# A one-core encoder layer in split precision: layer-norm fillers dealt anew, scratch sums on other memory, a fixed load order between up and down projection, and the last token tiles finished in halves

## The chip, the core and the metric

One core of one Trainium2 chip runs the whole layer. The metric is the device time of one execution in microseconds, the median of several. TensorE does the matrix products, VectorE (DVE), ScalarE (ACT) and GpSimd (POOL) the rest, and DMA queues, most of them SyncE's (SP), move data between the memories.

## What is computed

The reference is one layer of a streaming encoder for 1024 prompt tokens and 64 sample tokens of width 1024, in float32:

```python
u = x * (1.0 + sc1) + sh1
xr, gl, q, k, v, ga, gb = split(u @ w_in)              # 1024 -> 7 x 1024
y_a = RG_LRU(causal_conv4(xr)) * gelu(gl)
y_b = chunk_band_attention(q, k, v)
merged = sigmoid(ga) * y_a + sigmoid(gb) * y_b
x1 = LN(ALPHA * x + (1.0 + g1) * (merged @ w_out))
u2 = x1 * (1.0 + sc2) + sh2
f = square(relu(u2 @ w_up + b_up)) @ w_down + b_down   # 1024 -> 4096 -> 1024
y = LN(ALPHA * x1 + (1.0 + g2) * f)
```

The outputs are y of both token sets, the newest keys and values, and the recurrent states. The change touches what follows `merged`.

## The kernel before

Every matrix product is made of three: each operand is split into a high part (ACT, a copy to the rounded format) and a low part (VectorE, the difference), and `mm3` (lines 108 to 111) adds high by high, high by low and low by high. The tokens are cut into three groups: groups 0 and 1 of 384 prompt tokens, and group 2 of 256 prompt and 64 sample tokens (320 columns).

**First layer norm.** `outproj` (541) multiplies `merged` by w_out in eight blocks of 128 features. `ln1` (583) takes a group's three tiles of tokens: `ln1_a` transposes a tile (tile `rt`), makes its statistics and normalizes it on ACT (tile `n1`); `ln1_b` transposes it back (tile `nt`), makes u2 in high and low parts (`u2h`, `u2l`) and, on GpSimd, the part that the second norm adds (`nT`). Between the steps `fill(i)` puts other matmuls: the output projection of the next group, dealt by `cut` (642), and in group 2 the first blocks of the up projection, dealt by `early` (652). The power of -0.5 in the statistics (522) runs on GpSimd.

**Up projection.** 32 feature blocks go in 16 pairs. Pairs 0 and 1 are made within the layer norm, in plain form, their results in `hr`; pair 2 is plain too. From pair 3 on, groups 0 and 1 go through a Strassen scheme of seven products (`strassen`, 742) whose token operands are u2 and four sums of it, T1 to T4. These sums are made on VectorE in `tt` tiles (684 to 705): joins of high and low parts, subtractions, then splits into the T tiles. `wops` (708) makes the sums of weights on GpSimd and their splits. Group 2 is plain (`up_g2`, 754). For pairs 14 and 15 (`LATE`, 763) the second weight is split only in half, and group 2 is done after all pairs, with the weights loaded and split a second time (843 to 848).

**Down projection.** Results lie in DRAM (`hs_d` for the scheme, `hg_d` for group 2). `down_g2` (824) does group 2 for the first half of the features, then four passes c of the scheme run over seven operands each, then `down_g2` does the second half of group 2. Between its blocks stand the final norms of groups 0 and 1, one tile of tokens each (`final`, 885), and after it that of group 2.

Tiles take their memory in pools that are opened and closed; a new pool lies on the memory of closed ones, and each tile waits for those that lay there. The instructions of each engine are put in order by a planner with a timing model of its own; each engine, and each DMA queue, then takes them strictly in that order. `tc.issue_after(x)` queues the instructions of its block that run on x's engine behind x.

## Time and profile before

| | us |
|---|---|
| median of 3 runs (lowest, highest) | 1777.72 (1776.98, 1779.84) |
| the profiled execution, its own time | 1780.97 |
| its span, first to last instruction | 1779.0 |
| TensorE busy / weight loads busy | 1718.8 / 1682.1 |
| VectorE / ACT / GpSimd busy | 1012.8 / 771.4 / 457.4 |

In the profile a line names the engine, the source line, the operation and its tiles, written as out<-in. PE is TensorE, PEld its weight load. The granted clock is 1.00 at 2.4 GHz and 0.50 at 1.2 GHz; a stretch with both has a mean. A wait in brackets is the idle time of the engine ahead of the instruction and what ended it. Times within the execution are counted from its first instruction.

### The profile page before, as it was taken

The page shows a single profiled execution, that of the slowest core. Times are in us where ns is not written, and L with a number is a line of the kernel's source. Part 1 is how long each engine was busy: PE and PEld are TensorE (multiplying, and loading weights), DVE is VectorE, ACT ScalarE, POOL GpSimd, SP SyncE. Part 2 cuts the span into 40 slices and gives each one's busy share as a digit, 9 for nine tenths or more (in the row PEclk, how much of TensorE's full clock was granted, in tenths as well). Part 3 has the DMA queues.
Part 4 walks back from the last instruction along what each step waited for, and adds up shares of the span by engine and source line. Part 5 has one row for each costly group of instructions (what it writes and reads, how often), then busy time and mean ns, then how long its engine had stood idle before and what let it go on. Part 6 is the DMA issues. An engine that isn't in the chain of part 4 may idle for free.

```text
span 1779.0 us, 26773 instructions
## 1 busy us (share of the span) xinstructions
PE 1718.8 (97%) x10684; PEld 1682.1 (95%) x10684; DVE 1012.8 (57%) x1596; ACT 771.4 (43%) x1158; POOL 457.4 (26%) x487
## 2 busy tenths in 40 slices
PE   7999999999999999999999988999999899999996
PEld 4999999999999999999899888999998899999996
DVE  4594553746536374453656738333332567897876
ACT  2452543625244262443534444555555543344343
POOL 1100010000100000010025665556654024443313
PEclk8999999999999999999999999999999899999998
DMA  9241313122221122212154533333333973454343
GB/s 360 90 134 56 100 50 103 57 69 81 69 97 53 61 93 68 97 48 70 63 188 148 187 117 113 125 125 125 130 135 115 346 258 116 167 195 143 137 154 113
DMA packets 88253, 220.20 MB, mean 124 GB/s; under 512 B 11520, under 2 KB 42496, under 8 KB 88128
## 3 DMA queue, kind: packets, MB, share of 16 engines
q1 hardware_dynamic: 72512, 191.21, 31.8%
q10 hardware_dynamic: 11520, 14.69, 2.3%
q0 software_dynamic: 4096, 12.59, 1.9%
q8 instruction: 84, 1.38, 0.3%
q14 instruction: 41, 0.34, 0.1%
HBM read 173.62 MB, written 44.83 MB: 123 GB/s over the span
## 4 chain that ended last, share of the span: by engine, by line
PE 86%; DVE 5%; issue 3%; DMA 2%; ACT 2%; POOL 1%; SPq 0%; ACTq 0%; DVEq 0%; POOLq 0%
PE z L111 12%; PE z L110 12%; PE z L109 12%; PE po L402 3%; PE s L391 2%; PE xu L109 2%; PE xu L110 2%; PE xu L111 2%; PE dg L111 2%; PE dg L109 2%; PE dg L110 2%; PE xd L109 2%; PE ug L111 2%; PE xd L111 2%; PE ug L109 2%
## 5 line engine op out<-in xcount | busy, mean ns | idle before, releaser
L109 PE MATMUL z<-uh,wh_in 128*128 128x384 f32 (+1 forms) x1320 | 435.3, 330 | 2.9 <-ACT uh L102 2.9
L110 PE MATMUL z<-ul,wh_in 128*128 128x384 f32 (+1 forms) x1320 | 436.9, 331 | 0.3 <-DVE ul L103 0.3
L111 PE MATMUL z<-uh,wl_in 128*128 128x384 f32 (+1 forms) x1320 | 435.7, 330 | 0.0
L109 PEld LDWEIGHTS z<-uh,wh_in 128*128 128x128 f32 x1320 | 248.7, 188 | 6.3 <-ACT uh L102 3.9
L110 PEld LDWEIGHTS z<-ul,wh_in 128*128 128x128 f32 x1320 | 248.6, 188 | 4.4 <-DVE ul L103 2.3
L111 PEld LDWEIGHTS z<-uh,wl_in 128*128 128x128 f32 x1320 | 248.7, 188 | 4.0 <-issue 3.1
L96 ACT ACTIVATE wh_in<-wr_in 128x1024 fp32r<-128x1024 f32 x56 | 59.4, 1060 | 105.2 <-PE z L110 100.3
L97 DVE TENSOR_TENSOR wl_in<-wr_in,wh_in 128x1024 fp32r<-128x1024 f32 x56 | 68.5, 1223 | 43.2 <-ACT wh_in L96 43.1
L111 PE MATMUL dg<-ophg,wl_dg 128*128 128x320 f32 x256 | 79.3, 310 | 1.6 <-DVE wl_dg L97 1.6
L160 DVE SCALAR_TENSOR_TENSOR ap<-ar,sil,ap 128x512 f32<-128x512 f32 x112 | 79.7, 742 | 0.0
L109 PE MATMUL dg<-ophg,wh_dg 128*128 128x320 f32 x256 | 79.6, 311 | 0.0
L110 PE MATMUL dg<-oplg,wh_dg 128*128 128x320 f32 x256 | 79.1, 309 | 0.0
L451 POOL MEMSET er<- 128x1 f32 x8 | 1.1, 136 | 296.9 <-DVE rt L447 296.9
L103 DVE TENSOR_TENSOR slo_u<-sr_u,shi_u 128x1024 fp32r<-128x1024 f32 x26 | 33.0, 1267 | 65.9 <-ACT shi_u L102 65.9
L374 ACT ACTIVATE pr<-pr,st 128x640 f32<-128x640 f32 (+2 forms) x64 | 44.7, 699 | 57.7 <-DVE st L373 57.5
L103 DVE TENSOR_TENSOR opl<-op,oph 128x1536 fp32r<-128x1536 f32 x28 | 59.7, 2132 | 15.0 <-ACT oph L102 14.9
L357 DVE COPY v<-vt 128x512 f32<-128x512 f32 x16 | 11.1, 692 | 96.9 <-PE vt L356 96.9
L398 ACT ACTIVATE pts<-pt 128x512 f32<-128x512 f32 (+2 forms) x64 | 33.3, 520 | 74.2 <-PE pt L396 73.2
L102 ACT ACTIVATE shi_d<-sr_d 128x1024 fp32r<-128x1024 f32 x32 | 33.8, 1057 | 72.4 <-PE yd L110 49.7
L330 POOL TENSOR_TENSOR ko<-kh,kl 128x512 f32<-128x512 f32 x8 | 10.3, 1290 | 212.2 <-DVE kl L324 181.8
L402 PE MATMUL po<-pts,v 128*128 128x128 f32 x480 | 64.1, 275 | 0.5 <-ACT pts L398 0.3
L103 DVE TENSOR_TENSOR wlo_u<-wr_u,whi_u 128x1024 fp32r<-128x1024 f32 (+1 forms) x26 | 36.3, 1398 | 48.5 <-ACT whi_u L102 48.5
(372 smaller groups left out, 4707.9 us busy)
## 6 DMA issues: line engine op xcount, KB each, us to landing
wr_in<-in_w_in SPq DMA_DIRECT2D x56, 512.0 KB, 3.3
ar<-in_w_ada SPq DMA_DIRECT2D x46, 512.0 KB, 5.1
op<-hs_d SPq DMA_DIRECT2D x28, 768.0 KB, 5.0
wr_u<-in_w_up SPq DMA_DIRECT2D x37, 512.0 KB, 3.7
wr_dg<-in_w_down SPq DMA_DIRECT2D x32, 512.0 KB, 4.2
wr_d<-in_w_down SPq DMA_DIRECT2D x32, 512.0 KB, 4.3
wr_o<-in_w_out SPq DMA_DIRECT2D x24, 512.0 KB, 3.5
hs_d<-t POOLq DMA_DIRECT2D x64, 192.0 KB, 2.5
```

The lines of the kernel that those rows point to most:

```text
L96: S.activation(hi, raw, AF.Copy)
L97: V.tensor_tensor(lo, raw, hi.bitcast(F32), op=ALU.subtract)
L102: S.activation(hi, src, AF.Copy)
L103: V.tensor_tensor(lo, src, hi.bitcast(F32), op=ALU.subtract)
L109: TE.matmul(ps, wh, xh, start=first, stop=False, skip_group_check=more)
L110: TE.matmul(ps, wh, xl, start=False, stop=False, skip_group_check=more)
L111: TE.matmul(ps, wl, xh, start=False, stop=last, skip_group_check=more)
L160: V.scalar_tensor_tensor(part[:, w, :], raw[:, j, :], sil[:, kb, w:w + 1], part[:, w, :], op0=ALU.mult, op1=ALU.add)
L374: S.activation(pr[:rows, :W], pr[:rows, :W], AF.Exp, bias=st[:rows, 0:1], scale=-1.0, accum_out=st[:rows, 1:2])
L391: TE.matmul(sps[:, bk, :cw], qq[:, q0:q0 + P], kk[:, P * j0 + c0:P * j0 + c0 + cw], start=(ip == 0), stop=(ip == 2))
L398: S.activation(pts[:, :min(W, 512)], pt[:, :min(W, 512)], AF.Copy)
L402: TE.matmul(po[:, :P], v[:, j0 + j, :], pts[:, P * j:P * j + P], start=(j == 0), stop=(j == nk - 1))
```

## The change

1. `cut` and `early` deal the same blocks otherwise; the last piece of `early` is queued behind the last transpose of the layer norm.
2. The three `tt` tiles of the first half are asked for ahead of the T tiles, which changes the memory of both.
3. `LATE` is 15 and all weights are split whole. Pair 14 does its group 2 at once; pair 15 does it after the last product, with the weights it has. The loads around the start of the down projection are given an order, and the load of the last norm's factors goes behind the last operand.
4. In the passes of the down projection the weights of the first block are asked for ahead of the seven operands.
5. For the last three tiles of tokens the transposes and statistics of the first four features blocks are made within the last `down_g2`, three more blocks follow there, and the last one comes after it; the final operations are spread otherwise.

```diff
-        cut = ((0, 1), (2, 3), (4, 5), (6,), (7,))
+        cut = ((0,), (1, 2), (3, 4), (5, 6), (7,))
...
         def early(i):
-            for f in (ef[0:2], (), ef[2:4], ())[i] if i < 4 else ():
-                wt[f] = up_w(f)
-                up_mm(f, wt[f], 0)
-            for f in ((), ef[0:2], (), ef[2:3], ef[3:4])[i]:
-                up_mm(f, wt[f], 1)
-
-        ln1(2, rTs[2], early)
+            for k in ((0,), (1,), (2,), (3,), ())[i]:
+                wt[ef[k]] = up_w(ef[k])
+                up_mm(ef[k], wt[ef[k]], 0)
+            for k in ((), (0,), (1,), (2,), (3,))[i]:
+                up_mm(ef[k], wt[ef[k]], 1)
+
+        tail_of_ln = ln1(2, rTs[2], lambda i: early(i) if i < 4 else None)
+        with tc.issue_after(tail_of_ln):
+            early(4)
...
+        tts = [tt3(0)]
         ut = {}
...
-            x, y, z = (fp.tile([P, 2, GW], F32, tag="tt", bufs=3, name=f"tt{q}_{k}") for k in range(3))
+            x, y, z = tts.pop() if tts else tt3(q)
...
-        PLAIN, LATE = 3, 14
+        PLAIN, LATE = 3, 15
...
-            w, wa, wb = wops(a["w_up"][f1], a["w_up"][f2], f"u{p}_", p < LATE)
+            w, wa, wb = wops(a["w_up"][f1], a["w_up"][f2], f"u{p}_", True)
...
-            if p < LATE:
-                up_g2(p, wa, wb)
+            if p == LATE:
+                return wa, wb
+            up_g2(p, wa, wb)
...
         def down_g2(cs, hg, after):
...
-                        wh, wl = wsplit(a["w_down"][c, 4 * r + b], f"dg{r}_{c}_{b}")
+                        with tc.issue_after(loads[1]):
+                            wh, wl = wsplit(a["w_down"][c, 4 * r + b], f"dg{r}_{c}_{b}")
+                        if b == 1 and (c + 1, 0) not in hg and c + 1 in cs:
+                            with tc.issue_after(wlast[0]):
+                                hg.update({(c + 1, h): load_hg(c + 1, h) for h in range(2)})
+                            with tc.issue_after(loads[-1]):
+                                SY.dma_start(fg, facc_d[:, :, TS2:T])
...
-        wt = [up_w(f) for f in fblocks(LATE)]
         hg = {(0, h): load_hg(0, h) for h in range(2)}
         up_g2(LATE, *wt)
-        with tc.issue_after(loads[-1]):
-            for p in range(LATE + 1, 16):
-                up_g2(p, *(up_w(f) for f in fblocks(p)))
-        hg.update({(1, h): load_hg(1, h) for h in range(2)})
         fg = actb.tile([P, NB, TW2], F32, tag="act", bufs=2, name="fg")
-        SY.dma_start(fg, facc_d[:, :, TS2:T])
...
         for c in range(4):
-            ops = []
+            w, ops = down_w(c, 0), []
             for k in range(7):
                 o = hp.tile([P, 4, GW], F32, tag="opr", bufs=2, name=f"op{c}_{k}")
-                loads.append(SY.dma_start(o, hs_d[c, k]).ins)
+                with tc.issue_after(wloads[-1] if c == 0 and k > 4 else loads[-1]):
+                    loads.append(SY.dma_start(o, hs_d[c, k]).ins)
                 ops.append(op_split(o, f"{c}_{k}"))
...
+        with tc.issue_after(loads[-1]):
+            SY.dma_start(lg, a["ln2"][0].partition_broadcast(P))
+            SY.dma_start(lb, a["ln2"][1].partition_broadcast(P))
...
+        def final2():
+            lo, hi = halves
+            done = []
+            for c, cw, y, st, pt in g2t:
+                V.bn_stats(st[:cw, 1, :], pt[:cw, :])
+                done.append((c, cw, y, pt, *ln_moments(st, cw, f"b2_{c}")))
+            for c, cw, y, pt, mean, rstd, nb in done:
+                S.activation(y[:cw, lo], y[:cw, lo], AF.Identity, bias=nb, scale=rstd)
+                V.scalar_tensor_tensor(y[:cw, hi], pt[:cw, :], mean, lg[:cw, hi], op0=ALU.subtract, op1=ALU.mult)
+                (G if c == 0 else V).tensor_tensor(y[:cw, lo], y[:cw, lo], lg[:cw, lo], op=ALU.mult)
+                G.tensor_tensor(y[:cw, lo], y[:cw, lo], lb[:cw, lo], op=ALU.add)
+                V.scalar_tensor_tensor(y[:cw, hi], y[:cw, hi], rstd, lb[:cw, hi], op0=ALU.mult, op1=ALU.add)
+                SY.dma_start(a["y"][TS2 + c:TS2 + c + cw, :], y[:cw])
...
+        def between(r, c, b):
+            n = 8 * r + 4 * (c - 2) + b
+            if n % 2 == 1 and n < 12:
                 final(*next(fin))
+            if n == 13:
+                final2_open()
+            elif n == 14:
+                final2_more((4,))
+            elif n == 15:
+                final2_more((5, 6))
```

`final2_open` makes the transposes of feature blocks 0 to 3 of the last three tiles, their copy from the accumulators on ACT and the first half of the statistics; `final2_more(fbs)` adds the transposes of the blocks named, which `down_g2` has finished by then.

## Rows read from the trace of the kernel before

**Rows 1.** The page's busy time and share by engine.

```profile
PE 1718.8 (97%) x10684; PEld 1682.1 (95%) x10684; DVE 1012.8 (57%) x1596; ACT 771.4 (43%) x1158; POOL 457.4 (26%) x487
```

**Rows 2.** Stretches: length, busy time (instructions) by engine, PEclk, DMA share, GB/s.

```profile
1420.00:1440.00 20.00, 20.00 (x139) 20.00 (x138) 10.37 (x14) 6.80 (x7) 0.00 (x0) 1.00 0.75 264
1540.00:1560.00 20.00, 20.00 (x118) 20.00 (x117) 15.46 (x18) 5.92 (x7) 8.65 (x6) 1.00 0.30 102
988.90:996.00 7.10, 4.57 (x23) 4.38 (x22) 3.44 (x8) 3.18 (x3) 4.13 (x5) 0.76 0.62 213
1048.40:1057.20 8.80, 3.93 (x16) 3.91 (x16) 4.22 (x9) 1.64 (x3) 7.62 (x13) 0.61 0.25 80
1098.40:1109.00 10.60, 5.85 (x18) 5.09 (x19) 10.34 (x11) 6.11 (x10) 3.18 (x4) 0.68 0.44 145
1359.70:1371.00 11.30, 7.63 (x28) 6.80 (x27) 2.00 (x2) 4.55 (x8) 4.88 (x7) 0.70 0.29 104
1382.10:1395.00 12.90, 6.56 (x25) 5.90 (x24) 7.79 (x6) 9.05 (x10) 0.00 (x0) 0.60 0.83 298
1416.70:1418.60 1.90, 0.29 (x3) 0.03 (x2) 1.88 (x4) 1.52 (x2) 0.00 (x0) 1.00 0.89 350
1580.00:1640.00 60.00, 59.05 (x339) 58.35 (x338) 50.77 (x52) 25.03 (x23) 24.80 (x16) 1.00 0.47 162
```

**Rows 3.** Waits of TensorE: total us, times, longest.

```profile
PE up L109 <- ACT u2h L102: 6.3, 2, 4.9
...
PE xd L111 <- DVE wlo_d L103: 3.6, 3, 2.0
PE nt L572 <- ACT n L564: 3.2, 2, 2.5
...
PE xd L109 <- DVE facc L873: 2.5, 3, 0.9
```

**Rows 4.** Timeline (start us, us) behind the layer norm, and joins: ns min/median/max.

```profile
1047.71 0.71 PE L572 MATMUL nt<-ident,n 64*128 64x64 f32 x8
...
1053.27 0.73 DVE L103 TENSOR_TENSOR u2l<-uf,u2h 128x512 fp32r<-128x512 f32 x1 [0.69 <-ACT u2h L102]
1060.08 1.45 DVE L97 TENSOR_TENSOR wl_u<-wr_u,wh_u 128x1024 fp32r<-128x1024 f32 x1 [6.08 <-ACT wh_u L96]
...
1071.48 4.05 DVE L689 TENSOR_TENSOR tt<-u2h,u2l 128x768 f32<-128x768 f32 x2
...
L689 DVE TENSOR_TENSOR tt<-u2h,u2l x8: 945/2043/2082, 1071.5 to 1104.5; 128x768 f32<-128x768 f32 x8
```

**Rows 5.** Timeline of ACT around the last pair and the seam.

```profile
1359.91 1.06 ACT L96 ACTIVATE wh_u<-wr_u 128x1024 fp32r<-128x1024 f32 x1 [1.69 <-PE xu L110]
...
1362.55 0.49 ACT L782 ACTIVATE c<-xu 128x384 f32<-128x384 f32 x1 [0.56 <-ACT c L609]
...
1384.26 2.43 ACT L102 ACTIVATE ophg<-hg 128x1280 fp32r<-128x1280 f32 x2 [0.57 <-ACT cg L609]
```

**Rows 6.** The seam: SP's loads of hg, their landing, and TensorE's restart.

```profile
1373.33 0.82 SPq L821 DMA_DIRECT2D hg<-hg_d  x2
...
hg<-hg_d SPq DMA_DIRECT2D x2, 640.0 KB, 5.1
...
1387.69 0.63 PE L109 MATMUL ug<-u2h,wh_u 128*128 128x320 f32 x1 [5.28 <-ACT wh_u L96]
```

**Rows 7.** Timeline of the tail.

```profile
1754.73 2.42 POOL L901 TENSOR_TENSOR y<-y,lgb 128x1024 f32<-128x1024 f32 x1 [3.21 <-DVE y L900]
1760.10 2.78 PE L907 MATMUL yt<-ident,fg 128*128 128x128 f32 x24
1760.89 3.85 DVE L518 BATCH_NORM_STATS2 lstb<-yt 128x6 f32<-128x512 f32 x6
...
1768.94 1.71 POOL L901 TENSOR_TENSOR y<-y,lgb 128x512 f32<-128x512 f32 x1 [1.97 <-DVE y L900]
...
1773.49 0.68 DVE L901 TENSOR_TENSOR y<-y,lgb 64x512 f32<-64x512 f32 x1
```

More of the change, by code (lines that the diff above doesn't have):

```diff
@@ L515, in ln_stats, with ln_moments @@
             st = cpool.tile([P, 2, 6], F32, tag="lst", bufs=3, name=f"lst{nm}")
-            mv = cpool.tile([P, 6], F32, tag="lmv", bufs=3, name=f"lmv{nm}")
             for h in range(2):
                 V.bn_stats(st[:rows, h, :], ps[h][:rows, :])
+            return ln_moments(st, rows, nm)
+        def ln_moments(st, rows, nm):
+            mv = cpool.tile([P, 6], F32, tag="lmv", bufs=3, name=f"lmv{nm}")
             V.bn_aggr(mv[:rows, 0:2], flat(st[:rows]))
@@ L571, in ln1_b @@
             for fb in range(NB):
-                TE.transpose(pb[:, P * fb:P * fb + cw], n1[:cw, P * fb:P * fb + P], ident[:cw, :cw])
+                last = TE.transpose(pb[:, P * fb:P * fb + cw], n1[:cw, P * fb:P * fb + P], ident[:cw, :cw])
             nT = big([P, NB, cw], f"nT{g}_{c}")
@@ L581, in ln1_b @@
             SY.dma_start(facc_d[:, :, t0 + c:t0 + c + cw], nT)
+            return last.ins
         def ln1(g, rT, fill):
@@ L594, in ln1 @@
             fill(3)
-            ln1_b(g, n[2], *t[2])
+            last = ln1_b(g, n[2], *t[2])
             fill(4)
+            return last
         hraw = {}
@@ L678, in whole, with tt3 @@
             return x.bitcast(F32)
+        def tt3(q):
+            return [fp.tile([P, 2, GW], F32, tag="tt", bufs=3, name=f"tt{q}_{k}") for k in range(3)]
+        tts = [tt3(0)]
         ut = {}
@@ L706, in body @@
         uops = [b11, b21, ut[2], ut[1], ut[3], b22, ut[4]]
+        wloads, loads = [], []
         def wops(src1, src2, nm, full):
@@ L834, in down_g2, with down_w @@
                                 c == cs[0] and k == 0, c == cs[-1] and k == 7)
[L835 to L843 removed]
+                            if k == 4:
+                                after(r, c, b)
+                        if c == cs[-1]:
+                            fb = 4 * r + b
+                            for c0, c1, w in parts(2):
+                                fc = fg[:, fb, c0:c1]
+                                V.scalar_tensor_tensor(fc, ps[b][:, c0:c1], ada[:, G2, fb, w:w + 1], fc, op0=ALU.mult, op1=ALU.add)
         hg = {(0, h): load_hg(0, h) for h in range(2)}
         up_g2(LATE, *wt)
[L846 to L849 removed]
         fg = actb.tile([P, NB, TW2], F32, tag="act", bufs=2, name="fg")
[L851 to L852 removed]
+        down_g2((0, 1), hg, lambda r, c, b: None)
+        def down_w(c, j):
+            return wops(a["w_down"][c, 2 * j], a["w_down"][c, 2 * j + 1], f"d{c}_{j}", False)[0]
         for c in range(4):
[L855 removed]
+            w, ops = down_w(c, 0), []
             for k in range(7):
                 o = hp.tile([P, 4, GW], F32, tag="opr", bufs=2, name=f"op{c}_{k}")
[L858 removed]
+                with tc.issue_after(wloads[-1] if c == 0 and k > 4 else loads[-1]):
+                    loads.append(SY.dma_start(o, hs_d[c, k]).ins)
                 ops.append(op_split(o, f"{c}_{k}"))
@@ new lines, in body, with final @@
+        with tc.issue_after(loads[-1]):
+            SY.dma_start(lg, a["ln2"][0].partition_broadcast(P))
+            SY.dma_start(lb, a["ln2"][1].partition_broadcast(P))
+        halves = [slice(0, 512), slice(512, 1024)]
+        def final(g, i):
+            t0, tw = GROUPS[g]
+            c, cw = tok_tiles(g)[i]
+            pt = [acc(f"yt{g}_{c}_{h}") for h in range(2)]
+            for fb in range(NB):
+                TE.transpose(pt[fb // 4][:cw, P * (fb % 4):P * (fb % 4) + P], facc[fb][:, GW * g + c:GW * g + c + cw], ident)
+            y = hp.tile([P, D], F32, tag="sraw" if c < P else "slo", bufs=2, name=f"y{g}_{c}")
+            for h, s in enumerate(halves):
+                S.activation(y[:cw, s], pt[h][:cw, :], AF.Copy)
+            mean, rstd, nb = ln_stats([y[:, s] for s in halves], cw, f"b{g}_{c}")
+            S.activation(y[:cw], y[:cw], AF.Identity, bias=nb, scale=rstd)
+            V.tensor_tensor(y[:cw], y[:cw], lg[:cw], op=ALU.mult)
+            G.tensor_tensor(y[:cw], y[:cw], lb[:cw], op=ALU.add)
+            SY.dma_start(a["y"][t0 + c:t0 + c + cw, :], y[:cw])
@@ new lines, in body, with final2_open @@
+        g2t = []
+        def final2_open():
+            for c, cw in tok_tiles(2):
+                pt = acc(f"yt2_{c}_0")
+                for fb in range(4):
+                    TE.transpose(pt[:cw, P * fb:P * fb + P], fg[:, fb, c:c + cw], ident)
+                y = hp.tile([P, D], F32, tag="shi" if c < 2 * P else "opl", bufs=2 if c < 2 * P else 7, name=f"y2_{c}")
+                S.activation(y[:cw, halves[0]], pt[:cw, :], AF.Copy)
+                st = cpool.tile([P, 2, 6], F32, tag="lst", bufs=3, name=f"lst2_{c}")
+                V.bn_stats(st[:cw, 0, :], y[:cw, halves[0]])
+                g2t.append([c, cw, y, st])
@@ new lines, in final2_more @@
+        def final2_more(fbs):
+            for t in g2t:
+                c, cw = t[0:2]
+                if len(t) == 4:
+                    t.append(acc(f"yt2_{c}_1"))
+                for fb in fbs:
+                    TE.transpose(t[4][:cw, P * (fb - 4):P * (fb - 4) + P], fg[:, fb, c:c + cw], ident)
+        def final2():
[11 more added lines that the diff above has]
+                SY.dma_start(a["y"][TS2 + c:TS2 + c + cw, :], y[:cw])
@@ L932, in arrays_of @@
+        down_g2((2, 3), hg, between)
+        final2_more((7,))
+        final2()
 def arrays_of(i):
```

58 lines of the change are left out of this document (6 added, 52 removed).

## Prediction

> **What bounds the kernel now.** I read the page's totals first: TensorE is busy 97% of the span and its weight loads 95% [rows 1]. So the time is TensorE's own work plus its stops, and an edit on another engine is worth only what it takes from a stop. Then busy time by stretch [rows 2]. The first two rows give the full pitch: 20 us hold 139 matmuls of 320 columns, or 118 of 384, the ones cut by the edges counted whole; with two taken off, 0.146 and 0.172 us from one to the next. The other rows are the stops, which sit at the seams. The count of matmuls tells each loss: what that count takes at full pitch, taken from the length of the stretch.
>
> - 988.9 to 996.0: 8 transposes and some 15 matmuls, about 3.1 us of work in 7.1: 4.0 lost.
> - 1048.4 to 1057.2: 16 at 0.146 is 2.3 of 8.8: 6.5 lost.
> - 1098.4 to 1109.0: 18 at 0.172 is 3.1 of 10.6: 7.5 lost.
> - 1359.7 to 1371.0: 28 at 0.172 is 4.8 of 11.3: 6.5 lost.
> - 1382.1 to 1395.0: 25 at 0.146 is 3.7 of 12.9: 9.2 lost.
> - 1416.7 to 1418.6: 3 is 0.4 of 1.9: 1.5 lost.
>
> In all but the last the granted clock of the stretch is 0.60 to 0.76: behind these stops TensorE goes on for some microseconds at its lower level, 1.2 GHz, so a stop costs more than its idle time. The waits of TensorE add 6.1 us in the down projection (3.6 for weight remainders, 2.5 for VectorE's accumulations) and, in the first layer norm, 0.7 for n and 1.4 for u2h beside the long ones counted above [rows 3]. Together 43.4 us. Behind the last matmul stand 19 us of tail.
>
> **The change part by part.** All times are of the profiled execution: span 1779.0, its own time 1780.97, which is 3.25 above the median 1777.72. I subtract the sum from either.
>
> *Fillers, groups 0 and 1.* Eight blocks of the output projection are dealt 1, 2, 2, 2, 1 instead of 2, 2, 2, 1, 1. No instruction is added. Two blocks instead of one now stand ahead of the third tile's transposes, one block fewer ahead of the first tile's. The waits are for n and u2h [rows 3], 6.1 us in all. Both come out of a chain that passes through GpSimd's queue, and the change leaves that queue's work as it is, so I expect little: 1.5 gained, bounds -3.5 (a block of 24 matmuls at 0.146 missing ahead of the first tile) and 6.1.
>
> *Fillers, group 2.* Three of four blocks' matmuls are dealt one by one, and the last (24 matmuls of 384 columns, 4.1 us) is queued on TensorE behind the last transposes. In the trace those end at 1048.42 [rows 4] and TensorE then idles 4.9 us for u2h [rows 3], with the slow stretch behind. Work that doesn't hang on the last tile covers 4.1 of the 4.9; 0.8 idle should not lose the clock, since the 1.5 at 1416.7 did not. Gain 6.5 - 0.8 = 5.7; bounds 4.1 (the clock falls all the same) and 6.5.
>
> *Sums on other memory.* The three scratch tiles of the first half are asked for ahead of the eight T tiles, so they lie at the low end of the pool, where the layer norm's scratch (xa, n1) was, and not where the early blocks' results lay. In the trace VectorE sits idle 6.08 us ahead of 1060.08 and does weight remainders alone up to 1071.48, where the joins start, though the last of u2 was there at 1054.0 [rows 4]. From then to the last T split it is busy throughout, and TensorE waits for it: the 7.5 us. Eight joins at a median of 2.04 are 16 us; with as many subtractions and eight remainders of half a join's size or more I estimate 35 us of VectorE. Starting 10 to 15 us earlier in idle time they end ahead of the third pair. The T tiles move by 9 KB onto other results that are stored late; that may take some of the lead back. Gain 6.5, bounds 0 and 7.5.
>
> *Pair 14 regular, pair 15 keeps its weights.* LATE goes from 14 to 15 and the weights of both are split whole. Four loads of 512 KB, four ACT splits (1.06) and four VectorE remainders (1.2) go; two half splits (0.5 and 0.6) come per pair, under matmuls. At 1359.7 TensorE waits for the copy of pair 15's x (1362.55), which stands in ACT's queue behind the high part of a reloaded weight (1359.91, itself waiting for TensorE) and pair 14's last results [rows 5]. That weight split goes, and 48 matmuls of group 2 (7.0 us) stand between the two pairs, as in the pairs before, where no stop stands (from 1118 to 1342 TensorE waits for nothing). Gain 5.8 of 6.5, bounds 0 and 6.5.
>
> *The seam.* The wait of 5.3 for a reloaded weight goes with the reload. What is next: the first down matmul needs hg, and hg's load starts at 1373.33 [rows 6], when the memory of u2h of group 1 is read for the last time by pair 15; the change doesn't touch that. From there two loads land in 5.1 (median), two ACT splits take 2.43, the first weight's split 1.06 and its remainder 1.23: 9.8 us at best. TensorE holds 12 matmuls (2.1) and pair 15's group 2 (7.0): 9.1. That would leave 0.7. But in the trace ACT takes hg at 1384.26, behind the last group-2 results [rows 5], though by the median it had landed at 1378.4. With pair 15's results in the place of pair 14's, the same order gives the same restart, 14.4 us after the load [rows 6], and the same 9.2. And 7 us less of TensorE work covers the loads of hg, fg and the first weights. For it, the two lgb loads and the reloads no longer stand among them, and the order hg, two weights, hg, fg is fixed. I take the first stop as staying and the 1.5 at 1416.7 as going, with 0.5 more: gain 2.0, bounds -4 (one weight queued behind hg and fg late by one 24-matmul block) and 10.
>
> *Down projection.* Weights of j = 0 are queued ahead of the seven operands. VectorE is busy 50.8 of 60 us there [rows 2] (the last row), with peaks at each operand change. The order moves, the work stays: gain 2.0 of 6.1, bounds -2 and 6.1.
>
> *The tail.* 21 of 24 transposes move in among the matmuls; at 2.78 us for 24 [rows 7] that puts the last matmul 2.4 later. Three half tiles of statistics remain of six (3.85): 1.9 less. Then VectorE's rest falls by some 2.5 us, but GpSimd gets four operations of 512 columns in a row where it had two. One took 1.71 with VectorE beside it, 1024 columns took 2.42 without [rows 7]. So 4.8 to 6.8 us. I let them start at 1767.5: the first such operation of the trace, 1768.94, less two products of VectorE that it waited for, plus the later matmuls. They end at 1772.3 to 1774.3, against 1774.17 for VectorE's last of before. Gain 0.9, bounds -1 and 3. The Trainium skill (SBUF — State Buffer, SBUF: two separate sides) says that a VectorE operation with two SBUF inputs and a GpSimd one that reads SBUF exclude each other, the later one waiting whole: by it the slow figure holds wherever VectorE multiplies in SBUF, and the tail gains nothing; by the lone figure it gains 1.9. The trace's 1.71 agrees with the rule.
>
> Sum: 1.5 + 5.7 + 6.5 + 5.8 + 2.0 + 2.0 + 0.9 = 24.4. 1777.72 - 24.4 = 1753.3 (1756.6 for a run like the profiled one).
>
> **The rivals.** *The seam closes too.* If hg is split ahead of the last results, 8 more go at the seam, and with the weights early 3 more in the down projection: 1742. Against it: ACT's order in the trace. *The T tiles don't come earlier and the fillers of group 1 only move their wait*: 6.5 and 1.5 stay, 1761. For it: the T tiles' new memory also holds early results, which are stored late. *The planner deals the instructions by its own timing and most stops reappear elsewhere*: within 3 us of 1777.7. *VectorE's queue turns against TensorE, and it is slower.* With scratch memory free early, joins and T operations can stand ahead of the remainders of the weights that TensorE needs next. It has 24 matmuls at 0.172 and 72 at 0.146, 14.6 us, from the last transposes on; VectorE is free after 5.7 of them, so 9 us, or some six T operations of 1.5, fit. All 24 ahead cost 26 us, 2 more than the sum gains, with the clock lost again: 1782. It decides from some 22 operations on; the idle time ahead of the weight remainders [rows 4] speaks against so many.
>
> **How the numbers follow.** Forecast 0.56, own range 1746 to 1760. Seam closes: 0.14. T tiles late: 0.17. Nothing moves: 0.05. VectorE's queue: 0.08. Adding 0.2% (3.6 us, about what a measurement of this kernel can tell from no change) on either side of 1777.7: faster 0.56 + 0.14 + 0.17 = 0.87, same 0.05, slower 0.08. The range takes the first three, with the seam's and the down projection's bounds on the low side and the first part's and the seam's losses on the high side: 1739 to 1768.
>
> **What would show it.** No wait for u2h over 1 us behind the last transposes, and full clock there. Joins starting within 12 us of those transposes, no wait for T1l. No wait for the copy of x in the last pair. At the seam, the number that I trust least: how long after hg's load the first down matmul starts, 9 to 10 us or 14. In the down projection the waits for wlo. In the tail, GpSimd's last add against VectorE's last. Wrong would be: a new wait of TensorE for wl_u after the layer norm, or one for wl_dg several blocks into the down projection.

## The result, and the profile after

The changed kernel takes 1764.37 us (median; 1761.64 to 1767.86) against 1778.78 us of the kernel before, timed beside it: a ratio of 0.992, 95% interval 0.990 to 0.9941, so 14 us less. Forecast were 1753.3 us and 24.4 us less. The profiled execution of the changed kernel took 1761.64 us with a span of 1759.7, 2.7 below its median; the profiled one of before lies 2.2 above the median that holds here. So the spans differ by 19.3 us where the medians differ by 14.4, and what follows divides the 19.3.

The page's busy time by engine, after (before: [rows 1]). TensorE's busy time falls by 9.0 us: behind the stop at the seam a matmul of 320 columns is busy 0.47 to 0.64 us and at full clock 0.31, so time won back behind stops shows here too.

```profile
PE 1709.8 (97%) x10684; PEld 1674.2 (95%) x10684; DVE 1002.0 (57%) x1590; ACT 768.7 (44%) x1150; POOL 465.1 (26%) x489
```

TensorE's waits from 935 us to the end, after (total us, times, longest; before: [rows 3]). The wait for `u2h` is down from 6.3 to 0.8, that for `wlo_d` from 3.6 to 0.4. The wait for the high part of a weight at the seam is as long as it was: 5.2, now for `wh_dg`. The wait for `n` between the layer norm's steps is longer, 4.1 instead of 3.2.

```profile
PE dg L111 <- ACT wh_dg L98: 5.2, 1, 5.2
PE nt L577 <- ACT n L569: 4.1, 4, 2.1
PE yu L112 <- DVE T1l L105: 2.5, 1, 2.5
PE xd L111 <- DVE facc L894: 2.3, 3, 0.9
...
PE yu L111 <- ACT T1h L104: 1.0, 1, 1.0
PE up L111 <- ACT u2h L104: 0.8, 1, 0.8
...
PE xd L113 <- DVE wlo_d L105: 0.4, 1, 0.4
```

The stretches that answer to [rows 2] (length; busy time and count for PE, PEld, DVE, ACT, POOL; clock; DMA): the end of the layer norm, the T tiles, the last pair, the seam. The first and third run at full clock; the second and fourth still drop to 0.86 and 0.74.

```profile
1041.00:1050.00 9.00, 8.11 (x51) 7.26 (x50) 4.95 (x10) 3.22 (x6) 8.79 (x14) 1.00 0.32 102
1089.00:1101.00 12.00, 8.17 (x37) 7.19 (x36) 11.58 (x13) 6.59 (x12) 1.69 (x4) 0.86 0.53 166
1340.00:1366.00 26.00, 25.37 (x151) 25.05 (x151) 6.46 (x8) 12.02 (x23) 6.06 (x8) 1.00 0.20 71
1373.00:1386.00 13.00, 6.71 (x29) 6.04 (x28) 7.79 (x6) 8.54 (x10) 0.03 (x1) 0.74 0.82 287
```

As in the prediction, the loss of a stretch is its length less what its matmuls take at full pitch. At the seam: 29 matmuls less the two cut by the edges, 27 at 0.146 are 3.9 us of 13.0, so 9.1 are lost. Done in this way from matmul to matmul over the whole stage, and for the tail from the start of the 96th down matmul from the last to the end of the span:

| step | forecast gain | lost before, us | lost after, us | gain in the traces |
|---|---|---|---|---|
| fillers, groups 0 and 1 | 1.5 | 12.0 | 10.4 | 1.6 |
| fillers, group 2 | 5.7 | 8.1 | 3.2 | 4.9 |
| sums on other memory | 6.5 | 7.9 | 6.1 | 1.8 |
| pair 15 | 5.8 | 7.0 | 0.9 | 6.1 |
| seam | 2.0 | 11.5 | 9.2 | 2.3 |
| down projection, to 1660 us | 2.0 | 8.4 | 4.0 | 4.4 |
| tail (length) | 0.9 | 33.1 | 35.9 | -2.8 |

They add up to 18.3; the other 1.0 lies in places below 1 us. Two steps failed: the sums, and the tail. Two gains are less sure than the table looks. The line between the two rows of fillers is a choice: drawn at the last transposes of group 1, the first row loses as much after as before (10.0 and 9.9) and the second gains 6.6; only their sum, 6.5, doesn't depend on it. And the loss in the down projection varies by 3 us between traces of the same code (below).

**The T tiles.** VectorE's timeline, after. The joins (`tt<-u2h,u2l`) have their new memory and wait for nothing; yet they start at 1063.92, right behind the last of four weight remainders, which VectorE reached after waits of 4.7, 1.9, 2.2 and 2.3 us for their high parts.

```profile
1059.26 1.23 DVE L99 TENSOR_TENSOR wl_u<-wr_u,wh_u 128x1024 fp32r<-128x1024 f32 x1 [2.15 <-ACT wh_u L98]
1062.78 1.23 DVE L105 TENSOR_TENSOR wlo_u<-wr_u,whi_u 128x1024 fp32r<-128x1024 f32 x1 [2.30 <-ACT whi_u L104]
1063.92 2.69 DVE L702 TENSOR_TENSOR tt<-u2h,u2l 128x768 f32<-128x768 f32 x3
```

and some lines on, beside GpSimd's timeline of the same time:

```profile
1074.45 0.95 DVE L105 TENSOR_TENSOR T3l<-tt,T3h 128x768 fp32r<-128x768 f32 x1
1075.32 2.05 DVE L702 TENSOR_TENSOR tt<-u2h,u2l 128x768 f32<-128x768 f32 x1
...
1086.03 3.91 DVE L105 TENSOR_TENSOR T4l<-tt,T4h 128x768 fp32r<-128x768 f32 x1
```

```profile
1069.81 1.89 POOL L743 TENSOR_TENSOR sr_u<-wr_u,sr_u 128x512 f32<-128x512 f32 x1
1075.10 1.45 POOL L739 TENSOR_TENSOR sr_u<-wr_u 128x512 f32<-128x512 f32 x1 [3.39 <-DMA wr_u<-in_w_up]
1076.63 1.88 POOL L740 TENSOR_TENSOR sr_u<-sr_u,wr_u 128x512 f32<-128x512 f32 x1
1079.68 1.94 POOL L742 TENSOR_TENSOR sr_u<-wr_u,wr_u 128x512 f32<-128x512 f32 x1 [1.17 <-DVE slo_u L105]
```

An operation of VectorE that begins while GpSimd stands idle (1071.70 to 1075.10, 1078.51 to 1079.68) takes 0.95 us; beside GpSimd's sums the same one takes 2.05, and the one at 1086.03, beside three subtractions of GpSimd in a row, 3.91. From 1066.5 to 1089.9 nine operations together take 11.2 us longer than their undisturbed kind. TensorE is ready for T at 1090.4; the second half of `T1l` ends at 1094.7.

**The seam.** ScalarE's timeline, and the two loads of `hg` with their landing, after. `hg` had landed by 1370.6 (4.6 us, median, from issue); ScalarE takes it at 1375.88, behind the last group-2 results of pair 15, as forecast. From the load to the first down matmul (1379.31) it is 14.3 us, forecast 14.4.

```profile
1374.11 0.53 ACT L615 ACTIVATE cg<-ug,bup 128x320 f32<-128x320 f32 x1 [2.99 <-PE ug L113]
...
1375.88 2.43 ACT L104 ACTIVATE ophg<-hg 128x1280 fp32r<-128x1280 f32 x2 [0.53 <-ACT cg L616]
1378.22 2.93 ACT L98 ACTIVATE wh_dg<-wr_dg 128x1024 fp32r<-128x1024 f32 x3
```

```profile
1364.99 0.80 SPq L837 DMA_DIRECT2D hg<-hg_d  x2
```

**The tail.** VectorE's and GpSimd's timelines, and the line of the program's end with the duration of its operations in ns (min/median/max). A VectorE operation on one column of 64 rows takes 1.21 us instead of 0.14: it ends at 1748.15, when GpSimd's first product ends. GpSimd's four operations take 6.9 us and end at 1753.57, VectorE at 1750.0. Then GpSimd's drain, 8.83 us long and ending at 1758.9, holds the end: the last store had landed at 1756.6.

```profile
1746.94 1.21 DVE L528 SCALAR_TENSOR_TENSOR lmvb<-lmvb 64x1 f32<-64x1 f32 x1
```

```profile
1746.60 1.54 POOL L953 TENSOR_TENSOR y<-y,lgb 128x512 f32<-128x512 f32 x1 [1.22 <-ACT y L951]
1748.22 5.36 POOL L954 TENSOR_TENSOR y<-y,lgb 128x512 f32<-128x512 f32 x3
```

```profile
L1025 POOLq DRAIN  x3: 40/102/8832, 1750.1 to 1759.4; - x3
```

### The profile page after: what moved, and what is told of

Read it like the earlier page. It is cut to its first block, busy times and chain, and to the rows that moved or that the text cites. A ratio compares the mean times of both kernels' runs of the same rounds, so it can differ in the third digit from the quotient of the medians.

```text
span 1759.7 us, 26743 instructions
## 1 busy us (share of the span) xinstructions
PE 1709.8 (97%) x10684; PEld 1674.2 (95%) x10684; DVE 1002.0 (57%) x1590; ACT 768.7 (44%) x1150; POOL 465.1 (26%) x489
## 4 chain that ended last, share of the span: by engine, by line
PE 88%; DVE 5%; issue 2%; DMA 2%; ACT 1%; POOL 1%; SPq 0%; POOLq 0%; ACTq 0%; DVEq 0%
PE z L112 13%; PE z L113 13%; PE z L111 12%; PE po L404 3%; PE s L393 2%; PE dg L113 2%; PE dg L112 2%; PE dg L111 2%; PE xd L111 2%; PE xu L111 2%; PE xu L112 2%; PE xu L113 2%; PE xd L112 2%; PE xd L113 2%; PE ug L113 2%
## 5 line engine op out<-in xcount | busy, mean ns | idle before, releaser
L98 ACT ACTIVATE wh_in<-wr_in 128x1024 fp32r<-128x1024 f32 x56 | 59.3, 1060 | 105.3 <-PE z L112 100.3
L111 PE MATMUL ug<-u2h,whi_u 128*128 128x320 f32 x208 | 64.3, 309 | 0.0
```

Of the source, the lines that this page charges most:

```text
L98: S.activation(hi, raw, AF.Copy)
L111: TE.matmul(ps, wh, xh, start=first, stop=False, skip_group_check=more)
```

## The experiments

Ratios are to the kernel before, timed beside each; the changed kernel's is 0.992 (0.990 to 0.9941). Intervals are some 0.2% to either side, 3.5 us, so effects below that are read from the traces. In traces of the same code the loss at T lies between 5.9 and 7.4 us, that at the seam between 9.1 and 9.6.

### Does the memory of the sums do anything?

On the kernel before, the change's allocation alone:

```diff
+        tts = [tt3(0)]
         ut = {}
...
-            x, y, z = (fp.tile(... tag="tt" ...) for k in range(3))
+            x, y, z = tts.pop() if tts else tt3(q)
```

> The kernel before, with one part of the change alone: the scratch tiles of the first half of the sums on the layer norm's memory. As forecast: joins 10 us earlier than 1071.5, the stop of 7.5 us goes, 5 to 7.5 us faster than before. Theory now: the joins stand on VectorE behind four weight remainders whatever their memory, so they start within 1 us of 1071.5 and the stop stays within 1.5 us of 7.8; within 2 us of before.

Measured: 1780.97 us, ratio 1.0012 (1.0002 to 1.0021); 7.9 us lost at T, as before. The first join starts 1.1 us behind the start of the fourth remainder and thus directly after it (VectorE's timeline), and the joins' median is 2.043 us as in [rows 4].

```profile
1072.49 1.22 DVE L103 TENSOR_TENSOR wlo_u<-wr_u,whi_u 128x1024 fp32r<-128x1024 f32 x1 [2.30 <-ACT whi_u L102]
1073.63 5.98 DVE L693 TENSOR_TENSOR tt<-u2h,u2l 128x768 f32<-128x768 f32 x3
```

The edit gains nothing: with memory free the joins start no earlier behind the remainder, 2.1 us later in time as the whole stage is. What the run is slower by, 2 us, is lost ahead of this stage, in the layer norm (22.9 us from 940 to 1060 against 20.1), and is not explained here.

### Is it VectorE's order?

On the changed kernel, the joins of the first half ahead of pair 2's second weight. TensorE's order is pinned too (not shown), but to the order of the program's text. That isn't the order which the planner gives the changed kernel: there T1's product stands ahead of T2's, with group 2 of pair 3 between the products. So what the expectation says of TensorE's order, that it is held as it was, doesn't hold.

```diff
-            V.tensor_tensor(z, z, x, op=ALU.subtract)
+            sums_done = V.tensor_tensor(z, z, x, op=ALU.subtract).ins
+            if q == 0:
+                sums0 = sums_done
...
-                wa, wb = up_w(f1), up_w(f2)
+                wa = up_w(f1)
+                with tc.issue_after(sums0):
+                    wb = up_w(f2)
```

> The changed kernel, with the six joins and subtractions of the first half queued on VectorE ahead of the second weight's remainder of pair 2, and TensorE's order held as it was. In the changed kernel the joins have their memory early but start only at 1063.9, right behind four weight remainders, and TensorE loses 6 us at 1090 to 1098 waiting for T1. Theory A (the order on VectorE is what makes T late, the memory alone moved nothing): joins start near 1057, the stop at T1 goes, 4 to 6 us faster than the changed kernel (1758 to 1760, a span near 1754). Rival B (VectorE has too little time in all, whatever the order): the stop only moves to T4 or to the weights of pair 3 or 4, within 1.5 us of 1764. Rival C: the held-back remainder of pair 2's second weight stops TensorE, 1 to 4 us slower.

Measured: 1768.12 us, ratio 0.9943 (0.9924 to 0.9963): rival C. The joins start 5.7 us earlier, but the first remainder of T waits for ScalarE, and behind it pair 2's weight: TensorE stops 2.3 us for it, and then 4.4 us for a copy of x in ScalarE's queue (VectorE's timeline and TensorE's waits, of this kernel).

```profile
1069.58 2.08 DVE L105 TENSOR_TENSOR T1l<-tt,T1h 128x768 fp32r<-128x768 f32 x1 [6.01 <-ACT T1h L104]
```

```profile
PE xu L114 <- ACT c L810: 4.4, 1, 4.4
PE up L116 <- DVE wl_u L99: 2.3, 1, 2.3
```

The second half of T1 is done 2.0 us earlier than in the changed kernel (1092.67 against 1094.68), but TensorE, which now takes T2 first and has no group 2 to fill with, loses some 10 us in this stage instead of 6. As its order moved along with VectorE's, the run doesn't tell what the place on VectorE alone is worth; that ScalarE's high parts stand between the joins and T it does show (6.0 us of waiting for `T1h`). Whether another order of these engines would gain is left open.

### Is it GpSimd?

First, GpSimd's order: the sums of pair 4 behind the subtractions of pair 2 (`lastsub` holds the last of them). For this, pair 4's weights are asked for earlier in the program, and pair 3's subtractions go behind the sums (not shown); TensorE's order in this stage is the same as in the changed kernel.

```diff
-            G.tensor_tensor(t4, c21, t2, op=ALU.subtract)
+            lastsub[0] = G.tensor_tensor(t4, c21, t2, op=ALU.subtract).ins
...
+            if nm == "u4_":
+                with tc.issue_after(lastsub[0]):
+                    weight_sums()
+            else:
+                weight_sums()
```

> The changed kernel, with GpSimd's four sums for the weights of pair 4 queued behind its subtractions of pair 2 (they ran ahead, from 1075 to 1083.6); the orders of TensorE and of VectorE's T operations stay. In both kernels VectorE's joins and T operations take 0.95 us while GpSimd stands idle and about 2.05 us while it works, and the earlier run that moved the joins ahead on VectorE gained nothing. Theory A (GpSimd's sums between VectorE's operations set T's time): five T operations between 1075 and 1085 fall from 2.05 to 0.95, the second half of T1 is there near 1090 instead of 1094.7, the stop of 6 us falls below 2.5; 3 to 5 us faster than the changed kernel (1758.5 to 1760.5). Rival B (VectorE's order or ScalarE's high parts set it): the stop stays within 1.5 us of 6, and the time within 1.5 us of 1763.5.

Measured: 1766.09 us, ratio 0.9932 (0.9917 to 0.9947). The operations of the first half fall to 0.95 us as theory A says, but the sums now run from 1091 on, between those of the second half (VectorE's timeline):

```profile
1083.52 0.94 DVE L726 TENSOR_TENSOR tt<-tt,tt 128x768 f32<-128x768 f32 x1
...
1093.57 2.03 DVE L105 TENSOR_TENSOR T1l<-tt,T1h 128x768 fp32r<-128x768 f32 x1
1095.53 2.45 DVE L721 TENSOR_TENSOR tt<-tt,tt 128x768 f32<-128x768 f32 x1
```

Counted from the last transposes, the second half of T1 is done 2.6 us earlier, T2's at the same time. The wait for `T1l` falls from 2.5 to 1.2 us, a copy of x, which ScalarE does behind T2's high part, adds 2.2, and 5.5 us are lost instead of 6.1. By its numbers this is rival B; by its rows GpSimd's sums slow other operations instead. So the next run takes GpSimd out, for the eight weight sums of pairs 3 and 4 and the four subtractions of pair 2:

```diff
+            E = V if nm in ("u3_", "u4_") else G
...
-            G.tensor_tensor(s1, rb[:, h[0], :], rb[:, h[1], :], op=ALU.add)
+            E.tensor_tensor(s1, rb[:, h[0], :], rb[:, h[1], :], op=ALU.add)
...
+            E = V if p == 2 else G
-            G.tensor_tensor(t1, c12, c11, op=ALU.subtract)
+            E.tensor_tensor(t1, c12, c11, op=ALU.subtract)
```

> The changed kernel, with the eight weight sums of pairs 3 and 4 and the four subtractions of pair 2 on VectorE instead of GpSimd; the order of operations around them shifts with it. In the run that only held the sums back, the T operations of 1075 to 1085 fell from 2.05 to 0.95 us, but those of 1091 to 1098 rose to 2.03 to 2.45 where the sums then ran, and 5.5 us of the stop of 6 stayed. Theory A (what T loses is GpSimd's turn between VectorE's operations, wherever it falls): no T operation above 1.3 us, the twelve moved operations add 7 us to VectorE and give back some 11, the stop falls to 1 to 3.5 us; 2.5 to 5 us faster than the changed kernel (1758.5 to 1761). Rival B (VectorE's 34 operations are too many in this stage in any case): the stop stays above 4.5 us and the time within 1.5 us.

Measured: 1769.56 us, ratio 0.9954 (0.9939 to 0.997), slower than the changed kernel, though the loss at T is gone: 0.1 us. The eight joins, by their tile's rows (ns), TensorE's waits from 1040 to 1390, and, by the timelines of VectorE and TensorE, when the second half of `T1l` is made and when TensorE takes it (its sixth matmul of T1 and its eighth, the first that needs that half):

```profile
L703 DVE TENSOR_TENSOR tt<-u2h,u2l x8: 950/952/954, 1065.8 to 1095.8; 128x768 f32<-128x768 f32 x8
```

```profile
PE yu L111 <- ACT shi_u L104: 5.6, 11, 0.5
...
PE xu L111 <- ACT c L799: 2.3, 1, 2.3
```

```profile
1092.18 0.95 DVE L105 TENSOR_TENSOR T1l<-tt,T1h 128x768 fp32r<-128x768 f32 x1
```

```profile
1092.31 0.33 PE L113 MATMUL yu<-T1h,slo_u 128*128 128x384 f32 x1
...
1098.11 0.34 PE L112 MATMUL yu<-T1l,shi_u 128*128 128x384 f32 x1
```

Twelve operations more on VectorE (eight of 0.69, four of 0.55: 7.7 us), none of its T operations above 0.96 us, and the second half of T1 done 3.4 us earlier, counted from the last transposes: so far theory A. But that the whole stop is gone isn't shown to be GpSimd's doing, since the planner dealt TensorE's work anew as well. In the changed kernel TensorE takes the twelve matmuls of T1 in a row. Here it takes six, then group 2 and the first half of T2, and comes to the second half of `T1l` 5.8 us later. In the old order it would have asked for `T1l` near 1092.7, half a microsecond too early, and T2's second half is done only 0.7 us earlier than in the changed kernel, counted in the same way. How much of the 6 us the moved operations take away with TensorE's order held stays open. What was gained went elsewhere: the planner put the last products of one pair inside the next, TensorE asks for the high part of the weight sums 0.5 us too early in eleven pairs, 0.68 us lost each time (7.4 in all), and from the last pair to the first down blocks 3.8 more. Whether the order did that is told by the last run, below.

### The seam

On the changed kernel; `osplit` holds ScalarE's latest `hg` split.

```diff
-                relu2(c, ps[:, :TW2], f)
+                if p == LATE and b == 1:
+                    with tc.issue_after(osplit[0]):
+                        relu2(c, ps[:, :TW2], f)
+                else:
+                    relu2(c, ps[:, :TW2], f)
```

> The changed kernel, with one edit: ScalarE's two hg splits at the seam stand ahead of the last group-2 result of pair 15 instead of behind it. In the changed kernel hg has landed at 1370.6 but is split only at 1375.9, behind that result, and TensorE stops 5.2 us and then runs on at its lower clock. Theory A (ScalarE's order is the stop): splits at 1371 to 1374, the first down matmul 4 to 5 us earlier, 4 to 7 us faster than the changed kernel (1757 to 1760). Rival B (the weights or their remainders are next behind, all late by the same): 0 to 2 us faster.

Measured: 1760.5 us, ratio 0.9903 (0.9886 to 0.9921). ScalarE's timeline and TensorE's waits:

```profile
1373.05 2.44 ACT L838 ACTIVATE ophg<-hg 128x1280 fp32r<-128x1280 f32 x2 [0.40 <-ACT cg L616]
1375.39 0.51 ACT L615 ACTIVATE cg<-ug,bup 128x320 f32<-128x320 f32 x1
1375.80 1.04 ACT L98 ACTIVATE wh_dg<-wr_dg 128x1024 fp32r<-128x1024 f32 x1
```

```profile
PE dg L111 <- ACT wh_dg L98: 1.8, 1, 1.8
PE dg L113 <- DVE wl_dg L99: 1.0, 1, 1.0
```

The wait falls from 5.2 to 1.8, the time from the load of `hg` to the first down matmul from 14.3 to 10.9, the loss at the seam from 9.2 to 5.1. So ScalarE's order was most of the stop; behind it come the weight's own split and remainder. The gain, 4.1 us by the trace and 3 to 4 by the medians, is at the low end of theory A's 4 to 7, as 2.8 us of waits remain and the clock still falls (0.83 from 1374 to 1384).

### The tail

Three variants of the changed kernel: two of the three last additions on VectorE (the diff); these, the third and the product of the first tile too; and the tail of before.

```diff
-                G.tensor_tensor(y[:cw, lo], y[:cw, lo], lb[:cw, lo], op=ALU.add)
+                (G if c == 0 else V).tensor_tensor(y[:cw, lo], y[:cw, lo], lb[:cw, lo], op=ALU.add)
```

> The changed kernel, with the last additions of two of the three tiles of the tail moved from GpSimd to VectorE. In the changed kernel GpSimd does four 512-column operations in 6.9 us and ends last, at 1753.6, VectorE at 1750.0. Theory A (GpSimd's four operations are the tail's bound): GpSimd ends near 1749.7, VectorE near 1751.4, 2 to 2.5 us faster than the changed kernel (1762). Rival B (the two engines hold each other up in SBUF, so the work only changes places): within 0.7 us of 1764.

Measured: 1764.83 us, ratio 0.9926 (0.9909 to 0.9942); 34.85 us from the 96th-last matmul instead of 35.86: between the two theories, nearer to B. VectorE's timeline and GpSimd's:

```profile
1750.59 1.28 DVE L953 TENSOR_TENSOR y<-y,lgb 128x512 f32<-128x512 f32 x2
1751.80 1.28 DVE L954 TENSOR_TENSOR y<-y,lgb 128x512 f32<-128x512 f32 x2
```

```profile
1750.07 4.12 POOL L954 TENSOR_TENSOR y<-y,lgb 128x512 f32<-128x512 f32 x1
```

One addition of 512 columns takes 4.12 us on GpSimd: it goes on until 1.1 us behind the last of VectorE's four operations, about what such an addition takes alone (1.25, the last of the three at 1748.22). Those four aren't slowed: 0.64 each. The first tile's store waits for that addition, and the two others behind it in the queue; the last lands at 1759.37, and the end comes 1.15 us later.

> The changed kernel, with all products and additions of the tail on VectorE and none on GpSimd. With two of the three additions moved the lone addition left on GpSimd took 4.12 us and ended 1.1 us behind VectorE's last. Theory A (an operation of GpSimd in SBUF and VectorE's with two operands there exclude each other, so a step on GpSimd adds its whole 1.2 us to the pair's time where VectorE needs 0.63): from the 96th-last down matmul to the end 33.5 to 34.2 us instead of 35.86, 1.7 to 2.3 us faster than the changed kernel (1761.5). Rival B (the engines work beside each other, VectorE with six more operations becomes the last): no change or up to 1 us slower.

Measured: 1762.29 us, ratio 0.9907 (0.9892 to 0.9922); 32.64 us, a gain of 3.2 where theory A said 1.7 to 2.3. VectorE's six operations take 0.63 each; GpSimd's drain (6.30 us, begun at 1748.2) is over at 1754.5, 5.8 before the end, so it is the last store that ends the program: the end comes 1.14 us behind its landing. By that measure the changed kernel's drain held its end 1.9 us longer than its stores would have. Theory A lacked this part:

```profile
1751.45 1.88 DVE L953 TENSOR_TENSOR y<-y,lgb 128x512 f32<-128x512 f32 x3
1753.25 1.88 DVE L954 TENSOR_TENSOR y<-y,lgb 128x512 f32<-128x512 f32 x3
```

```profile
L1025 POOLq DRAIN  x3: 40/93/6304, 1748.2 to 1760.0; - x3
```

> The changed kernel with the tail of before for group 2: all 24 transposes and all six half-tile statistics behind the last matmul, results kept in PSUM. Theory A (the new tail is a loss: from the last down matmul to the end 19.5 us after, 18.9 before, with 21 transposes, 2.4 us, moved in front of it): 2 to 4 us faster than the changed kernel (1760.5 to 1762.5). Rival B (as forecast, the new tail gains 0.9): 0.5 to 2 us slower than the changed kernel.

Measured: 1761.96 us, ratio 0.9911 (0.9896 to 0.9926); 32.99 us from the 96th-last matmul, 2.9 less than in the changed kernel and within 0.1 of before. So the new tail is a loss of 2.8 us, by a row that doesn't depend on what the rest of a run did; the medians show 2.4, less than their intervals.

### What the pairs, the seam and the down projection give alone

On the kernel before: these parts of the change, with the fillers, the sums and the tail left as they were.

> The kernel before, with the pairs 14 and 15, the seam and the order of the down projection as in the change, and with the fillers, the memory of the sums and the tail as before. Theory: these carry most of the gain. Stage by stage in the two traces they gave 6.1 (pair 15), 2.3 (seam) and 4.4 (down projection), so 11 to 14 us faster than before (1764 to 1767). Rival: pair 15 alone counts and the rest came from the other parts' shift, 5 to 8 us faster.

Measured: 1769.45 us, ratio 0.9945 (0.9928 to 0.9962): 10 us less, just under the theory's 11 to 14, and by the spans 11.5. Pair 15 loses 0.9 and the seam 9.4, about as in the changed kernel; the down projection 6.0 instead of 8.4. TensorE's waits from 935 to 1660 us:

```profile
PE up L111 <- ACT u2h L104: 6.3, 2, 4.9
PE dg L111 <- ACT wh_dg L98: 5.3, 1, 5.3
...
PE xd L113 <- DVE wlo_d L105: 1.9, 2, 1.6
```

And the changed kernel with the load order of the down projection as before:

```diff
-            w, ops = down_w(c, 0), []
+            ops = []
...
-                with tc.issue_after(wloads[-1] if c == 0 and k > 4 else loads[-1]):
-                    loads.append(SY.dma_start(o, hs_d[c, k]).ins)
+                loads.append(SY.dma_start(o, hs_d[c, k]).ins)
```

> The changed kernel, with the loads of the down projection's first phase queued as in before: a chunk's seven operands first, then the weights of its first block. Theory A (the order of the loads is what took TensorE's waits for weight remainders from 3.6 to 0.4 us): the stops at the operand changes come back, 8.4 us of excess instead of 4.0 between 1460 and 1660; 3 to 5 us slower than the changed kernel (1766.5 to 1768.5). Rival B (the stops shrank since the earlier stages ended at other times): within 1.5 us of the changed kernel.

Measured: 1765.45 us, ratio 0.9929 (0.991 to 0.9948). The waits for `wlo_d` come back to 1.3 us and the loss from 1440 to 1660 to 5.7: 1.7 of the 4.4 us, so rival B by its time. But traces of the same code differ by more than that. From the first of the projection's 1308 matmuls to the one behind the last it takes 229.7 to 232.7 us in the eleven traces with the new order (230.7 in the changed kernel), and with the old one 232.4 here, 233.9 with the sums alone and 235.1 before. What separates the two orders in every trace is one stop, 9 us into the projection: 2.2 us before, 0.7 and 0.6 in the other two, none with the new order. So the order gains something like 0.6 to 2.2 us; the rest of the 4.4 is how the earlier stages end, and chance.

### Together

The changed kernel with ScalarE's order at the seam, the transposes of the tail as before, and all products and additions of the tail on VectorE:

> The changed kernel with ScalarE's hg splits ahead of the last group-2 result, the transposes of the tail all behind the last matmul as in before, and its products and additions all on VectorE. If the parts add: 3 to 4 us for the seam as measured; for the tail, where all on VectorE gave 35.86 to 32.64 us from the 96th-last down matmul to the end with 21 transposes moved in front, and the old order 32.99 with two additions on GpSimd that VectorE waited 2.2 us for, I expect 32.0 to 32.7; together 6 to 8 us faster than the changed kernel (1755.5 to 1758). If the tail's parts overlap: 1758 to 1760.

Measured: 1755.06 us, ratio 0.9872 (0.9856 to 0.9889), its interval clear of the changed kernel's and a little under the 1755.5 to 1758 expected: the parts add. The seam loses 5.0 us, the tail takes 31.25 us, less than the 32.0 to 32.7 expected. To this the twelve operations on VectorE, with TensorE's order pinned (`prev` holds the last product of the pair before):

```diff
+                with tc.issue_after(prev[0]):
+                    strassen(w, uops, f"u{p}", after)
```

> The kernel with the seam's and the tail's edits, and the twelve operations of pairs 2 to 4 on VectorE instead of GpSimd as in the run before; now each later pair's seven products on TensorE are queued behind the seven of the pair before. In the run with the twelve operations alone the stop for T fell from 6.06 to 0.11 us, but from pair 4 on TensorE's order had the last products of one pair inside the next, 0.68 us was lost once a pair (9.7 in all) and 3.8 more at the seam. Theory A (those losses came from that order, not from the moved operations): the stop for T stays below 1 us, nothing is lost from 1110 to 1340 us, the seam as in the kernel without the moved operations; 4 to 6 us faster than that kernel (1749 to 1751.5). Rival B (the moved operations themselves leave VectorE or ScalarE behind in the later pairs): the 0.68 us a pair comes back, 1758 or more.

Measured: 1753.69 us, ratio 0.9855 (0.9833 to 0.9876): not told apart from the run before, and above the 1749 to 1751.5 expected. The 0.68 us a pair (my 9.7 for all of them was too high) is gone, so that loss was the order, theory A. But the stop for T isn't below 1 us: TensorE now waits 2.0 us for a copy of x in pair 3, since no product of group 2 stands between, and 1.3 us more are lost around the last pair and the seam. The run has TensorE's order of the run with the twelve operations up to that point, so it doesn't tell either what they are worth with the changed kernel's order.

```profile
PE xu L113 <- ACT c L810: 2.6, 2, 2.0
```

It is the fastest median of all, 1.4% below the kernel before.

## Why the prediction was right, and where it wasn't

The direction, the range (1739 to 1768) and the steps that carry most of the gain held. The point was 11 us too low: 1764.4 lies above the forecast's own 1746 to 1760, nearest to the rival "T tiles late" (1761). Of the 11 us, the sums account for 4.7 and the tail for 3.7; the down projection gave 2.4 more than forecast; and 4.9 are by how much the medians differ less than the two profiled executions.

- **Fillers.** 1.5 and 5.7 forecast, 1.6 and 4.9 in the traces; the sum is shown, the 1.5 for groups 0 and 1 is not, as it comes and goes with where the line is drawn, and in traces of the same code that loss varies by 2 us. Behind the last transposes TensorE idles 0.8 us at full clock, as worked out. In the trace of the run with the late parts alone the fillers' stages lose what they lost before.
- **Sums on other memory.** 6.5 forecast, nothing by the run that makes this edit alone; where the 1.8 us less in the changed kernel's trace come from is open. The joins start 22 us behind the last transposes, not within the 12 that I gave as a sign, against 23 before. The step that failed is "starting 10 to 15 us earlier in idle time". [Rows 4] already showed the joins right behind the weight remainders; I read VectorE's idle time ahead of a remainder as room for joins, though VectorE works in the order of its queue and the remainder ahead of them was waiting for ScalarE. I put the joins' place down to memory without a row that shows them wait for it. What the runs show in its place: the joins stand behind four remainders, whose high parts come late from ScalarE, and GpSimd's sums then and subtractions then lengthen nine of VectorE's operations by 11.2 us. How much of TensorE's stop that makes is open. The second mistake: I took 2.04 us as the price of a join. Its minimum in the same row is 0.945; 2.04 is the price beside GpSimd. The rival "T tiles late" had the effect, and a wrong cause.
- **Pair 15 and the seam.** 5.8 and 2.0 forecast, 6.1 and 2.3 in the traces; the stop that I expected to stay stayed, for the reason given: ScalarE's order. The rival "seam closes too" is what the run with that order changed makes of it, in part: 4.1 of the 8 us.
- **Down projection.** 2.0 forecast, 4.4 in the trace, 2.4 with the late parts alone, 1.7 given back by the old order. That the gain was twice the forecast is in part luck of these two traces: the same code differs by 3 us from one to the next.
- **Tail.** A gain of 0.9 forecast, a loss of 2.8 measured, inside neither of my bounds (-1 to 3). Three terms: GpSimd's first operation starts 1.2 us later than I let it, behind VectorE's products of other tiles; its four operations take 6.9 us, above the slow end of 4.8 to 6.8; and the end is set by GpSimd, not by VectorE's last. In the trace of before, too, GpSimd's last operation ends at 1772.9 and the span 6.1 us later, though VectorE's last ends at 1774.17. I compared with the wrong engine, which hid 1.3 us.

The Trainium skill (SBUF — State Buffer, SBUF: two separate sides) calls the port pair that VectorE with two SBUF inputs shares with a GpSimd operation that reads SBUF an exclusive lock, held for the whole operation. I weighed it at the tail alone. The runs agree with it there (4.12 us for an addition that needs 1.25) and at T, where I had not looked for it: 2.05 us for operations of 0.95. What the runs show beyond it is who comes next where both have work: at T the two engines mostly take turns one by one, but one remainder (3.91 us) spans three subtractions of GpSimd, and in the tail GpSimd's addition spans VectorE's operations in a row.

## What to carry to other kernels

Before an operation is given room or memory to start earlier, read what stands ahead of it in its own engine's queue and what that one waits for; idle time in front of a waiting instruction is no room. Where one kind of operation has two durations in one trace, look at what the neighbour engine does in the long ones: here work moved from GpSimd to VectorE costs VectorE 0.55 to 0.69 us and frees it of 1.1. And a stop removed shows its gain only if the planner keeps its order elsewhere; compare the order of TensorE's work in both programs before believing a time, or the cause of a stop that is gone. Before a microsecond or two of one trace is put down to an edit, see how much that stage varies in traces that share its code.

## What the runs showed of the hardware that I had not expected

- GpSimd's drain at the program's end. In all fourteen traces it ends 5.32 us after GpSimd's last operation (whose end the profile gives roughly). In ten of the eleven whose tail keeps such an operation late the span ends 6.1 us after that operation (6.09 to 6.11). In the other four, where the drain is over before the last store has landed or just behind it, the end comes 1.14 to 1.15 us after that landing. So in this kernel GpSimd holds the end where its last operation ends less than some 5 us (6.10 less 1.14) before the last store lands.
- VectorE and GpSimd: 2.05 us instead of 0.95 while they take turns, 3.91 beside three operations of GpSimd, 1.21 instead of 0.14 for a single column, and 4.12 instead of 1.25 for GpSimd beside VectorE's operations in a row.
- The 0.5 us waits, eleven times over, in the pairs of the kernel with the sums on VectorE left the clock at 1.0, as the 0.8 at 1046 and the 2.0 in pair 3 of the last run did; the stops at T (1.0 and 2.5 us) and at the seam (5.2, or 1.8 and 1.0) did not (0.86, 0.74, 0.83).
